# Gate stage of a streaming encoder layer: rows turned by VectorE, h added by accumulating loads, and a pair's finishing placed inside the next pair

## The chip, the cores and the metric

The kernel runs on one core of a Trainium2 chip. The metric is the device time in microseconds of one execution; the figure of a kernel is the median of its runs. A profile is one further execution, recorded by the hardware. The engines of the core are named as in the profile: PE (TensorE, matrix products; PEld its weight loads), DVE (VectorE), ACT (ScalarE), POOL (GpSimd) and SP (SyncE, which here only issues transfers). Each engine works through its own list of instructions in order and waits where an instruction needs another engine's result or a transfer.

## The reference

One layer for 2048 frames of a new stream and 32 frames of a running one, 1024 channels each, in fp32:

```
hn   = rmsnorm(x, g_mix);  proj = hn @ w_in
h    = x + concat(mixer_A(proj), mixer_B(proj)) @ w_out
gate = sigmoid(rmsnorm(h, g_ple) @ w_ple_gate)        # 1024 x 1024
h    = h + (p @ w_ple) * gate                         # p: 256 wide
y    = rmsnorm(h, g_final)
```

The change concerns only the last three lines, the gate stage, from the stored h to the result y.

## The kernel before

Frames lie in 16 tiles of 128 rows and a short one of 32 (`tiles`). Earlier stages leave three things in device memory: `h_d`, the rows h; `e_d`, the rows e = p @ w_ple (for tile 15 e is computed in the gate stage itself); and `g_d`, the gate's weights, already scaled by g_ple. The factor 1/rms of each row is kept on chip (`rs_h`) and goes in as the scale of the sigmoid.

The gate product works on **pairs** of tiles, eight pairs (i = 0, 2, ... 14; "pair one" is i = 0, "pair eight" is i = 14 and has its own function `last_pair`). Two tiles of rows are the upper and lower half of a 2 x 2 block matrix, the channels its left and right half, and the product with the 2 x 2 blocks of the weights is formed with seven block products in place of eight (Strassen-Winograd, function `seven`). The operands on the rows' side are four blocks of the turned rows (channels on the partitions) and four sums:

- a11, a12: left and right half of the upper tile; a21, a22: of the lower tile
- S1 = a21 + a22, S2 = S1 - a11, S3 = a11 - a21, S4 = a12 - S2

Each operand is split into a part that PE takes at its full rate (`fp32r`, cast by ACT, line 77: "the cast") and the rest (`subtract` on DVE, line 78: "the low part"). A block product is 12 matmuls of 128 x 512: four chunks of channels times three combinations of parts. `seven` runs them in the order 11, 12, S2, S1, S3, S4, 22 (the last is called T4 after its weight block) into three banks X, Y and Z: 11, S2, S3 and 22 all add on in bank X, S1 and S4 in Z, 12 in Y.

What is done with a bank between two products is given to `seven` as two functions, `carry` and `out` (`gate_ops`). `carry` copies a bank to SBUF (ACT, line 1302), `out` adds a copy to a bank (DVE, line 1310), applies the sigmoid (ACT), multiplies with e (DVE, line 1313) and adds to h (DVE, line 1314). Since X goes on being written, the next product into X has to wait until the copy or the addition from X is done; between a product into X and the next there is always a product into another bank. The places are named (tile, half): X gives (0,0) after 11 and 12, (1,1) after S3, (1,0) after T4; Z gives (0,1) after S4.

`done_g` finishes a tile: sum of squares by ACT (line 88), two steps on POOL for 1/rms (`rstd_of`, lines 69 and 73), scaling by DVE (line 1321), and the transfer of the rows to y, issued by POOL (line 1322). It is called after both tiles of the pair are through.

The rows' side of the next pair is prepared by `prep_g` in two steps that `seven` calls between its products. The two tiles of a pair are turned in two ways:

- upper tile, `turned`: rows loaded, re-ordered by ACT (two copies `ho`, line 1280), turned by PE in eight transposes of 128 x 128 into the two `tr` banks (`pth`, line 1282)
- lower tile, `turned_here`: loaded as 4 x 4 KB blocks by four transfers (line 1291) and turned in blocks of 32 x 32 by one DVE transpose (line 1293); the blocks are laid so that this gives whole columns

Loads go out on SP's queue. Rings of buffers: `xh` (three tiles of rows), `ya` (five), `cmb` (eight split operands, seven per pair), `st` (carries), `qa` (`ho`). A load waits for the last reader of its buffer, and all loads behind it on SP's queue with it. The framework that records the kernel orders the instructions of each engine by due times of its own, within their dependences: the lists that result differ from the order of the calls, and a small change can move instructions some distance away.

Ahead of pair one come the last products of e (line 102, tiles e_3 to e_16), beside which DVE and ACT form the sums of the gate's weights chunk by chunk (`weight_sums`, loads at line 1268, `wg_r`), and the short tile (`plain`, "gl"), whose rows are turned by PE as well (`pth_16`, low parts `gl`).

Of the kernel before, what the change touches and what calls it, by code (L numbers as in the profile page):

```python
# [12 lines left out]
ALU = mybir.AluOpType  # L13
PSUM = bass.MemoryType.PSUM

P = 128
# [10 lines left out]
NT = SEQ // P + 1  # L27
NH = D // 2
# [6 lines left out]
def trunk(ctx, tc, x_p, x_s, c_conv, c_pool, p_p, p_s, g_mix, w_in, conv_w, conv_b, pool_w,  # L35
          pool_scale, w_out, g_ple, w_gate, w_ple, g_fin, y_p, y_s, sc_p, sp_p, sc_s, sp_s):
    nc = tc.nc
# [6 lines left out]
    h_d = tc.dram_tile([T, D], F32, name="h_d")  # L44
# [41 lines left out]
    def sumsq(x, n, name, r=None, later=False):  # L86
        ssq = sm.tile([P, 1], F32, tag="ssq", name=f"ssq_{name}")
        ins = nc.scalar.activation(junk[:n], x[:n], AF.Square, accum_out=ssq[:n])  # L88
# [218 lines left out]
    def ring4(t, name):  # L307
        return t.tile([P, D], F32, tag="t", name=name)
# [15 lines left out]
    def load_rows(pool, name, i, pr, sa=None):  # L324
        r, n = tiles[i]
        t = ring4(pool, f"{name}_{i}")
        nc.sync.dma_start(t[:n], pr[r:r + n] if sa is None else rows_of(pr, sa, r, n))
        return t

    with ExitStack() as s1:  # L330
# [17 lines left out]
        def put(piece, src):  # L348

            split(piece[:, :, 0], piece[:, :, 1], src)  # L350
# [274 lines left out]
        second = second_block()  # L625
# [475 lines left out]
    with ExitStack() as s2:  # L1101
# [13 lines left out]
        def half_of(x, at, n=P):  # L1115
            return x[at[0]][:n, at[1] * NH:at[1] * NH + NH]
# [145 lines left out]
        W = sums_slots("wg")  # L1262
# [9 lines left out]
        def turned(i):  # L1272

            r, n = tiles[i]
            t = load_rows(ya, "hn", i, h_d).rearrange("p (q k c) -> p k q c", q=4, k=KC)
            out = []
            for half in range(2):
                pt = tbank(f"pth_{i}_{half}")
                o = qa.tile([P, KH, P], F32, tag="q", name=f"ho_{i}_{half}")
                nc.scalar.copy(o[:n].rearrange("p k (q c) -> p k q c", q=4), t[:n, half * KH:half * KH + KH])  # L1280
                for k in range(KH):
                    nc.tensor.transpose(pt[:, k * P:k * P + n], o[:n, k], ident[:n, :n])
                out.append(pt.rearrange("p (k t) -> p k t", k=KH))
            return out

        def turned_here(i):
# [6 lines left out]
            nc.vector.transpose(t, t)  # L1293
            u = t.rearrange("p (g k t) -> p k g t", g=4, k=KC)
            return u[:, :KH], u[:, KH:]

        def gate_ops(h, e, n, name, i):
            scale = lambda at: rs_h[:n, i + at[0]:i + at[0] + 1]

            def carry(ps, at):  # L1300
                t = st.tile([P, NH], F32, tag="t", name=f"c_{name}_{at[0]}{at[1]}")
                nc.scalar.copy(t[:n], ps[:n])
                return t

            def out(ps, c, at):
                if c is None:
                    c = st.tile([P, NH], F32, tag="t", name=f"g_{name}_{at[0]}{at[1]}")
                    nc.scalar.activation(c[:n], ps[:n], AF.Sigmoid, scale=scale(at))
                else:
                    nc.vector.tensor_tensor(c[:n], ps[:n], c[:n], op=ALU.add)  # L1310
                    nc.scalar.activation(c[:n], c[:n], AF.Sigmoid, scale=scale(at))
                ee, hh = half_of(e, at, n), half_of(h, at, n)
                nc.vector.tensor_tensor(ee, ee, c[:n], op=ALU.mult)
                nc.vector.tensor_tensor(hh, hh, ee, op=ALU.add)

            return carry, out

        def done_g(i, h):
            r, n = tiles[i]
            rf = sumsq(h, n, f"f{i}")  # L1320
            nc.vector.scalar_tensor_tensor(h[:n], h[:n], rf[:n], g_bc[:n], op0=ALU.mult, op1=ALU.mult)  # L1321
            nc.gpsimd.dma_start(rows_of(y_p, y_s, r, n), h[:n])

# [18 lines left out]
        def last_pair(i, A):  # L1342
# [63 lines left out]
            def second(half, m):  # L1406
                ps = bank(f"e_l{half}")
                embed_product(ps, pps, wp, slice(half * NH, half * NH + NH))
                finish(1, half, ps, m)

            pps = embedded()
            seven(f"g{i}", A, W, carry, out, {5: lambda: second(1, NH)}, first_tile=True)
            second(0, NH // 2)

        def prep_g(i):

            A = {}
# [12 lines left out]

            def first():
                lower.extend(turned_here(i + 1))

            def second():
                a21, a22 = lower
                s1 = comb("S1", a21, a22, ALU.add, whole)
                a11, a12 = turned(i)
                put("11", a11)
                s2 = comb("S2", s1, a11, ALU.subtract)
                s3 = comb("S3", whole(a11), a21, ALU.subtract, whole)  # L1440
                put("12", a12)
                put("S2", s2)
                s4 = comb("S4", a12, s2, ALU.subtract)
# [8 lines left out]
        S = {}  # L1452
        n = tiles[NT - 1][1]
        A = short("gl", turned(NT - 1), n)
        for step in prep_g(0).values():
            step()
        for c in range(len(rest_e) - LATE, len(rest_e)):
            run(c)
        h, e = (load_rows(*a) for a in ((xh, "h", NT - 1, h_d), (ya, "e", NT - 1, e_d)))
        plain("gl", A, W, n, *short_ops(h, e, n))  # L1460
        done_g(NT - 1, h)
        for i in range(0, NT - 3, 2):
            A = S.pop(i)
            h = [load_rows(xh, "h", i + b, h_d) for b in range(2)]
            e = [load_rows(ya, "e", i + b, e_d) for b in range(2)]
            seven(f"g{i}", A, W, *gate_ops(h, e, P, f"g{i}", i), prep_g(i + 2))
            for b in range(2):
                done_g(i + b, h[b])
        last_pair(NT - 3, S[NT - 3])


# [27 lines left out]
```

## Time and profile before

| | us |
|---|---|
| median of 3 runs (lowest to highest) | 945.34 (943.99 to 947.28) |
| the profiled execution, its own time | 942.12 |
| its span, first to last instruction | 940.3 |
| PE busy | 920.7 |
| DVE busy | 726.3 |
| ACT busy | 480.5 |
| POOL busy | 126.2 |
| gate pairs, from the first product to PE's last (windows) | 770.6 to 932.3 |

The span is what the profile can explain; the time lies about 1.8 us above it. Mean granted PE clock was 0.994. In the profile's rows, the columns are start, duration, engine, line, operation, and what was written from what; `x12` counts equal instructions; in brackets stands the engine's idle time before, and who ended it. In rows of groups it is busy time, mean ns, and idle time before. Windows give for each engine busy time and number of instructions, then PE's clock, the share of the transfer engines and GB/s.

### The profile page before, as it was taken

To read this page: it belongs to the slowest core of one execution; us is meant where nothing else is said; L and a number is where in the kernel's file an instruction comes from. 1 tells how busy PE (TensorE), PEld (TensorE's weight loads), DVE (VectorE), ACT (ScalarE), POOL (GpSimd) and SP (SyncE) were. 2 spreads that over 40 slices of the span, in tenths; PEclk is the share of its full clock that TensorE was granted. 3 is DMA by queue.
4 is the path that set the end of the run, shared out by engine and by line. 5 is a ranking of instruction groups with operands and counts; after the bars stand their busy time and mean duration, and the time that the engine had idled before them with its cause. 6 is when DMAs were issued, how large, how long until landed. Compare 5 with 4: busy or idle time off the path is not lost.

```text
span 940.3 us, 13055 instructions
## 1 busy us (share of the span) xinstructions
PE 920.7 (98%) x4599; PEld 831.5 (88%) x4599; DVE 726.3 (77%) x1230; ACT 480.5 (51%) x890; POOL 126.2 (13%) x244
## 2 busy tenths in 40 slices
PE   7999999999999999999999999999999999999996
PEld 5999999999999999999999987888878868888885
DVE  6697998899587978785777588765554797888985
ACT  5554555454444554443454356334334875555564
POOL 2101222120000110000000010211211001211113
PEclk8999999999999999999999999999999999999999
DMA  8336586696952655418655359865785883566653
GB/s 247 101 105 172 143 243 197 182 255 207 423 166 80 178 161 144 151 52 287 198 167 176 117 176 305 263 194 170 217 253 171 307 274 130 201 227 209 216 207 112
DMA packets 133214, 182.96 MB, mean 195 GB/s; under 512 B 11164, under 2 KB 105116, under 8 KB 131869
## 3 DMA queue, kind: packets, MB, share of 16 engines
q1 hardware_dynamic: 117165, 131.70, 45.2%
q0 software_dynamic: 13248, 44.93, 14.9%
q10 hardware_dynamic: 2736, 5.51, 1.8%
q8 instruction: 36, 0.59, 0.3%
q14 instruction: 29, 0.24, 0.1%
HBM read 127.23 MB, written 54.86 MB: 194 GB/s over the span
## 4 chain that ended last, share of the span: by engine, by line
PE 74%; DMA 3%; DVE 2%; ACT 2%; issue 0%; POOL 0%; POOLq 0%; DVEq 0%; ACTq 0%
PE x_o L167 9%; PE x_g L167 9%; PE e L102 5%; PE z_g L167 5%; PE x_zab L556 5%; PE z_o L167 4%; PE x_ch L556 4%; PE x_zbv L556 4%; PE z_zab L556 2%; PE y_g L167 2%; PE y_o L167 2%; PE b L556 2%; PE v L556 2%; PE zb L556 2%; PE za L556 2%; PE c L556 2%
## 5 line engine op out<-in xcount | busy, mean ns | idle before, releaser
L77 ACT CAST y_S<-y_fS 128x512 fp32r<-128x512 f32 x32 | 19.5, 621 | 42.5 <-PE x_o L167 18.9
L102 PE MATMUL e<-wq,pps 128*128 128x512 f32 (+1 forms) x156 | 38.8, 399 | 0.2 <-ACT pps L77 0.2
L406 DVE SCALAR_TENSOR_TENSOR xt<-xt,rstd_x,g_bc 128x1024 f32<-128x1024 f32 (+2 forms) x18 | 23.1, 1282 | 19.4 <-POOL rstd_x L73 18.0
L167 PE MATMUL x_g<-wg_b,g_S 128*128 128x512 f32 x128 | 35.9, 390 | 0.0
L167 PE MATMUL x_o<-wo_b,y_S 128*128 128x512 f32 x128 | 35.8, 391 | 0.0
L556 PE MATMUL z_ch<-B,w_ch_S 128*128 128x416 f32 x168 | 34.3, 352 | 0.9 <-ACT U L851 0.9
L556 PE MATMUL z_zab<-B,w_zab_S 128*128 128x416 f32 x168 | 34.1, 351 | 0.5 <-ACT U L851 0.5
L556 PE MATMUL x_zab<-B,w_zab_S 128*128 128x416 f32 x168 | 34.5, 352 | 0.1
L556 PE MATMUL z_zbv<-B,w_zbv_S 128*128 128x416 f32 x168 | 34.2, 352 | 0.0
L556 PE MATMUL x_zbv<-B,w_zbv_S 128*128 128x416 f32 x168 | 34.1, 351 | 0.0
L556 PE MATMUL x_ch<-B,w_ch_S 128*128 128x416 f32 x168 | 34.0, 351 | 0.0
L102 PEld LDWEIGHTS e<-wq,pps 128*128 128x128 f32 (+1 forms) x156 | 27.4, 182 | 6.9 <-ACT pps L77 0.5
L556 PEld LDWEIGHTS z_ch<-B,w_ch_S 128*128 128x128 f32 x168 | 31.2, 188 | 1.6 <-ACT U L851 1.2
L556 PEld LDWEIGHTS z_zab<-B,w_zab_S 128*128 128x128 f32 x168 | 31.3, 188 | 1.1 <-ACT U L851 0.8
L556 PEld LDWEIGHTS x_zab<-B,w_zab_S 128*128 128x128 f32 x168 | 31.2, 188 | 1.0 <-DVE w_zab_S L78 0.4
L556 PEld LDWEIGHTS x_ch<-B,w_ch_S 128*128 128x128 f32 x168 | 31.4, 188 | 0.3
L556 PEld LDWEIGHTS x_zbv<-B,w_zbv_S 128*128 128x128 f32 x168 | 31.3, 188 | 0.3
L556 PEld LDWEIGHTS z_zbv<-B,w_zbv_S 128*128 128x128 f32 x168 | 31.3, 188 | 0.4
L69 POOL TENSOR_SCALAR ms_f<-ssq_f 128x1 f32<-128x1 f32 (+1 forms) x15 | 8.8, 585 | 160.7 <-ACT junk L88 160.7
L77 ACT CAST y<-y 128x512 fp32r<-128x512 f32 x24 | 14.8, 618 | 29.4 <-PE x_o L167 13.8
L1321 DVE SCALAR_TENSOR_TENSOR h<-h,rstd_f,g_bc 128x1024 f32<-128x1024 f32 (+1 forms) x15 | 19.3, 1284 | 12.7 <-POOL rstd_f L73 12.7
L167 PEld LDWEIGHTS x_o<-wo_b,y_S 128*128 128x128 f32 x128 | 24.0, 188 | 5.0 <-ACT c_o L1125 0.3
(570 smaller groups left out, 2670.7 us busy)
## 6 DMA issues: line engine op xcount, KB each, us to landing
y<-y_d SPq DMA_DIRECT2D x16, 512.0 KB, 12.7
x<-in_x_prompt_dram SPq DMA_DIRECT2D x16, 512.0 KB, 9.7
h_d<-x SPq DMA_DIRECT2D x16, 512.0 KB, 4.5
h<-h_d SPq DMA_DIRECT2D x16, 512.0 KB, 3.6
xt<-in_x_prompt_dram SPq DMA_DIRECT2D x15, 512.0 KB, 12.7
e<-e_d SPq DMA_DIRECT2D x15, 512.0 KB, 5.9
out_dram<-h POOLq DMA_DIRECT2D x14, 512.0 KB, 3.0
p_dT<-T POOLq DMA_DIRECT2D x12, 512.0 KB, 6.2
```

Of the source, the lines that this page charges most:

```text
L69: nc.gpsimd.tensor_scalar(ms[:n], ssq[:n], scalar1=1.0 / D, scalar2=EPS, op0=ALU.mult, op1=ALU.add)
L77: ins = nc.scalar.copy(hi, src)
L102: nc.tensor.matmul(ps[:n], pps[:, a, k, :n], wp[k][b][:, cs], start=k + q == 0, stop=k == 1 and q == 2)
L167: nc.tensor.matmul(ps[:n], lhs[:, k, a, :n], w[b][:, k], start=start and k + q == 0, stop=k == KH - 1 and q == 2, skip_group_check=True)
L406: nc.vector.scalar_tensor_tensor(xt[:n], xt[:n], r[:n], g_bc[:n], op0=ALU.mult, op1=ALU.mult)
L556: nc.tensor.matmul(ps[:, :NB], lhs[:, k, x], b[:, k, y], start=start and k + q == 0, stop=stop and k == KH - 1 and q == 2, skip_group_chec ...
L1321: nc.vector.scalar_tensor_tensor(h[:n], h[:n], rf[:n], g_bc[:n], op0=ALU.mult, op1=ALU.mult)
```

## The change

Three things are done.

1. In pairs two to eight both tiles are loaded as blocks and turned by DVE (`blocks`, `turned_here`); only pair one (`here=False`) and the short tile keep PE's transposes. The block loads of both tiles are issued ahead of the loads of e, into ring `xh`.
2. h is no longer loaded for pairs one to seven. After the multiplication e x gate, h is added to the half tile by a transfer from `h_d` that adds to what lies in SBUF, issued by POOL (four per pair). The sums stand in the e tile then. The short tile and the last pair add h by DVE as before.
3. `done_g` of a pair is called inside the next pair, after its product S1 (step 4; in the last pair too).

```diff
+        def blocks(i):
             r, n = tiles[i]
-            t = ring4(ya, f"hn_{i}")
+            t = ring4(xh, f"hn_{i}")
             for q in range(4):
                 nc.sync.dma_start(...)
+            return t
+
+        def turned_here(t):
             nc.vector.transpose(t, t)
...
-                ee, hh = half_of(e, at, n), half_of(h, at, n)
+                ee = half_of(e, at, n)
                 nc.vector.tensor_tensor(ee, ee, c[:n], op=ALU.mult)
-                nc.vector.tensor_tensor(hh, hh, ee, op=ALU.add)
+                if h is None:
+                    r = tiles[i + at[0]][0]
+                    nc.gpsimd.dma_start(ee, h_d[r:r + P, at[1] * NH:at[1] * NH + NH], accum_op=ALU.add)
+                else:
+                    hh = half_of(h, at, n)
+                    nc.vector.tensor_tensor(hh, hh, ee, op=ALU.add)
...
-            rf = sumsq(h, n, f"f{i}")
+            rf = sumsq(h, n, f"f{i}", later=i < NT - 1)
...
-            seven(f"g{i}", A, W, carry, out, {5: lambda: second(1, NH)}, first_tile=True)
+            seven(f"g{i}", A, W, carry, out, {4: finished, 5: lambda: second(1, NH)}, first_tile=True)
...
-        def prep_g(i):
+        def prep_g(i, here=True):
...
-            lower = []
+            rows = [blocks(i + b) for b in range(1 - here, 2)]
+            upper = []
             def first():
-                lower.extend(turned_here(i + 1))
+                upper.extend(turned_here(rows[0]) if here else map(whole, turned(i)))
             def second():
-                a21, a22 = lower
+                a11, a12 = upper
+                put("11", a11, whole)
+                a21, a22 = turned_here(rows[-1])
                 s1 = comb("S1", a21, a22, ALU.add, whole)
-                a11, a12 = turned(i)
-                put("11", a11)
-                s2 = comb("S2", s1, a11, ALU.subtract)
-                s3 = comb("S3", whole(a11), a21, ALU.subtract, whole)
-                put("12", a12)
+                put("12", a12, whole)
+                s2 = comb("S2", whole(s1), a11, ALU.subtract, whole)
+                s3 = comb("S3", a11, a21, ALU.subtract, whole)
...
+        ready = []
+
+        def finished():
+            while ready:
+                done_g(*ready.pop(0))
+
         for i in range(0, NT - 3, 2):
             A = S.pop(i)
-            h = [load_rows(xh, "h", i + b, h_d) for b in range(2)]
+            steps = prep_g(i + 2)
             e = [load_rows(ya, "e", i + b, e_d) for b in range(2)]
-            seven(f"g{i}", A, W, *gate_ops(h, e, P, f"g{i}", i), prep_g(i + 2))
-            for b in range(2):
-                done_g(i + b, h[b])
+            seven(f"g{i}", A, W, *gate_ops(None, e, P, f"g{i}", i), {**steps, 4: finished})
+            ready.extend((i + b, e[b]) for b in range(2))
         last_pair(NT - 3, S[NT - 3])
```

In the changed kernel the lines lie some nine further down: the addition to a bank is line 1314, the multiplication 1317, the accumulating load 1320, the scaling 1330, the transfer to y 1331.

More of the change, by code (lines that the diff above doesn't have):

```diff
@@ L1284, in turned @@
             return out
-        def turned_here(i):
+        def blocks(i):
             r, n = tiles[i]
-            t = ring4(ya, f"hn_{i}")
+            t = ring4(xh, f"hn_{i}")
             for q in range(4):
@@ L1427, in comb @@
                 return t
-            lower = []
+            rows = [blocks(i + b) for b in range(1 - here, 2)]
+            upper = []
             def first():
-                lower.extend(turned_here(i + 1))
+                upper.extend(turned_here(rows[0]) if here else map(whole, turned(i)))
             def second():
-                a21, a22 = lower
+                a11, a12 = upper
+                put("11", a11, whole)
+                a21, a22 = turned_here(rows[-1])
                 s1 = comb("S1", a21, a22, ALU.add, whole)
-                a11, a12 = turned(i)
-                put("11", a11)
-                s2 = comb("S2", s1, a11, ALU.subtract)
-                s3 = comb("S3", whole(a11), a21, ALU.subtract, whole)
-                put("12", a12)
+                put("12", a12, whole)
+                s2 = comb("S2", whole(s1), a11, ALU.subtract, whole)
+                s3 = comb("S3", a11, a21, ALU.subtract, whole)
                 put("S2", s2)
-                s4 = comb("S4", a12, s2, ALU.subtract)
+                s4 = comb("S4", a12, whole(s2), ALU.subtract, whole)
                 put("S1", s1)
@@ L1454, in trunk @@
         A = short("gl", turned(NT - 1), n)
-        for step in prep_g(0).values():
+        for step in prep_g(0, here=False).values():
             step()
```

## The prediction

> **What bounds the kernel now.** I read the page's busy times, then the chain that ended last, then windows of the gate stage, then one pair's timeline.
>
> ```profile
> span 940.3 us, 13055 instructions
> PE 920.7 (98%) x4599; PEld 831.5 (88%) x4599; DVE 726.3 (77%) x1230; ACT 480.5 (51%) x890; POOL 126.2 (13%) x244
> 827.73:847.67 19.94, 19.94 (x94) 16.60 (x93) 17.43 (x27) 11.39 (x20) 3.36 (x6) 1.00 0.63 216
> 841.34 2.72 PE x_g L167 x12
> 844.06 0.68 PE z_g L167 x3
> 844.74 0.87 PE pth L1282 x8
> 845.62 2.06 PE z_g L167 x9
> ```
>
> TensorE (PE) is busy 98% of the span. In the gate stage it never pauses: in the window of one pair (19.94 us) PE is busy 19.94, VectorE (DVE) 17.43, ScalarE (ACT) 11.39, GpSimd (POOL) 3.36. The chain shows what a pair is: seven products of 2.72 us (19.04) and eight transposes `pth` of 0.87 us together. So PE sets the end here, and an edit pays by what it takes from PE, and costs by each wait that it gives PE. The profiled execution took 942.12 us, the median of the runs is 945.34; I form the change on the profiled run and put it on the median.
>
> **What is removed.** Pairs two to eight lose their `pth`: 7 x 0.87 = 6.1 us off PE, all on the path. This is the whole gain.
>
> ```profile
> L1280 ACT COPY ho<-hn 128x512 f32<-128x512 f32 x2 | 1.1, 622 | 0.0
> L1293 DVE STREAM_TRANSPOSE hn<-hn 128x1024 f32<-128x1024 f32 x1 | 1.2, 1236 | 0.0
> L1314 DVE TENSOR_TENSOR h<-h,e 128x512 f32<-128x512 f32 x4 | 2.7, 685 | 0.0
> hn<-h_d SPq DMA_DIRECT2D x24, 128.0 KB, 2.8
> out_dram<-hg POOLq DMA_DIRECT2D x1, 256.0 KB, 2.6
> L1322 POOL DMA_DIRECT2D out_dram<-h x2 | 1.1, 570 | 1.1 <-DVE h L1321 1.1
> ```
>
> Off the path, per pair: ACT loses two `ho` copies (1.1 us). DVE gains one transpose (1.2) and loses four additions (2.7). The loads of h (2 x 512 KB) give way to four accumulating loads of 256 KB, the row loads of the upper tile to block loads like the lower tile's, so about the same bytes move. POOL gains four issues of about 0.57 us (2.3 on 3.4 busy in some 20). None of these engines becomes the bound.
>
> The accumulating load is in no row. I take 2.6 us, POOL's other 256 KB transfer; the ends are 2.6 and 12.7, the slowest 512 KB load:
>
> ```profile
> y<-y_d SPq DMA_DIRECT2D x16, 512.0 KB, 12.7
> ```
>
> The last of a pair waits for the product T4 of that pair, a sigmoid and a multiplication: 2.7 + 0.2 + 0.7 + 0.7 and the issue of 0.57, some 5 us after T4 starts. The second sum of squares that reads it starts 15 us after T4 does (2.7 for T4, 1.8 for the rest of "11", three products, and 2.4, below). So 10 us are open to it, and up to there it costs nothing; nor can it gain, as no PE work is taken away by it. On POOL's queue an accumulating load waits for its multiplication; the one for half (0,0), the only one ahead of the means and roots, has its data 5 us before the first of these is due.
>
> **What is moved: the finishing of a pair.** This costs the time. In the instruction lists of the two kernels, each engine's order is fixed. Before, the squares (L88), POOL's root and the final scaling on DVE (L1321) run early in the next pair, ahead of that pair's addition for tile (1,1) (L1310). Now they are called after product S1, and in pairs four to seven the lists read:
>
> ```
> ACT   S3 cast (waits for PE: its buffer held S1)   carry of Z   squares   squares   S4 cast ...
> DVE   ... S3 low   scaling   scaling   S4 low   addition (1,1)   addition (0,1) ...
> PE    S1 | S3 | S4 | 4 matmuls of the next "11" | T4 (waits for addition (1,1), which reads its bank X)
> ```
>
> PE is in order, so T4 now waits behind two scalings. The price comes from the same steps in the trace before:
>
> ```profile
> 816.47 1.06 ACT L88 ACTIVATE junk<-h 128x1024 bf16<-128x1024 f32 x1 [1.96 <-DVE h L1314]
> 817.72 0.19 POOL L69 TENSOR_SCALAR ms_f<-ssq_f 128x1 f32<-128x1 f32 x1 [14.98 <-ACT junk L88]
> 818.58 1.28 DVE L1321 SCALAR_TENSOR_TENSOR h<-h,rstd_f,g_bc 128x1024 f32<-128x1024 f32 x1 [0.94 <-POOL rstd_f L73]
> 818.89 1.02 POOL L69 TENSOR_SCALAR ms_f<-ssq_f 128x1 f32<-128x1 f32 x1 [0.35 <-ACT junk L88]
> 820.58 1.29 DVE L1321 SCALAR_TENSOR_TENSOR h<-h,rstd_f,g_bc 128x1024 f32<-128x1024 f32 x1 [0.72 <-POOL rstd_f L73]
> 821.21 2.88 PE L167 MATMUL x_g<-wg_b,g_S 128*128 128x512 f32 x12
> 821.41 0.59 ACT L1302 COPY c_g<-z_g 128x512 f32<-128x512 f32 x1 [1.52 <-PE z_g L167]
> 821.78 0.69 DVE L1313 TENSOR_TENSOR e<-e,c_g 128x512 f32<-128x512 f32 x1
> 821.89 1.14 ACT L1280 COPY ho<-hn 128x512 f32<-128x512 f32 x2
> 784.29 0.69 DVE L1310 TENSOR_TENSOR c_g<-x_g,c_g 128x512 f32<-128x512 f32 x1 [1.26 <-PE x_g L167]
> 785.02 0.72 ACT L1311 ACTIVATE c_g<-c_g,rs_h 128x512 f32<-128x512 f32 x1 [1.84 <-DVE c_g L1310]
> 808.75 1.88 DVE L78 TENSOR_TENSOR g_S<-g_fS,g_S 128x512 fp32r<-128x512 f32 x3
> ```
>
> Let s be the end of S1 (the S3 product starts at 821.21). ACT reacts 0.20 later. S3 cast and carry take about 0.5 each (821.41 to 821.89 for one copy), so squares start at s + 1.2. From the first square to the second scaling: 816.47 to 820.58 = 4.11; that scaling holds DVE until 821.78, 1.20 more: s + 6.5. S4's low part takes 0.6 of DVE's queue (three in 1.88), the addition until its reader starts 0.73 (784.29 to 785.02): T4 may start at s + 7.84. PE has for cover S3, S4 and four matmuls: 2.72 + 2.72 + 0.91 = 6.35. PE waits 1.5 us in each of four pairs: **6.0**. Each pair starts from the last one's delay, and the steps in front (casts, first carry) have slack of over 2 us, so the wait neither grows nor is made up. It is 0.7 at least, if POOL's step `ms_f` takes 0.19 as at 817.72 and not 1.02; 2.3 if each of its two steps loses that 0.83 again.
>
> Here a row and a rule meet. `ms_f` takes 0.19 with DVE waiting and 1.02 under a scaling. The Trainium skill (SBUF — State Buffer, "Who interferes with whom") says that a VectorE instruction with two SBUF inputs contends with a GpSimd instruction that reads SBUF, and the 1.02 agrees. By the rule the 1.02 stays, since the same scaling runs beside it; without it the four waits would fall to 2.8 us in all.
>
> Pair two finishes pair one in another order: no cast ahead (squares at s + 0.7), but three forming steps (0.6 each) between scalings and addition, two of them behind the second. Scaling two ends at s + 6.0 to 6.3, the two steps 1.2, the addition 0.73: 8.0 to 8.2, against 2.72 + 2.72 + eight matmuls 1.81 = 7.25: **0.9** (0 to 1.5). Pair three has 12 + 6 matmuls ahead of T4, a cover of 9.5. Its second scaling stands behind four steps of DVE: first scaling s + 2.8 to 4.0, four steps to 6.4, scaling to 7.6, two steps to 8.8, addition 9.5: just in time, **0.3** (0 to 1).
>
> The finished rows now leave later too, and an e buffer of the 5-deep ring with them:
>
> ```profile
> out_dram<-h POOLq DMA_DIRECT2D x14, 512.0 KB, 3.0
> ```
>
> Issued at s + 5.9, landed at s + 8.9; there SP's load of a later e waits for the buffer, and behind it on SP's queue the four block loads of the next tile to be turned. These land by about s + 13.8 (2.1 to issue five, 2.8). DVE comes to that transpose after the next pair's product 12 and its first multiplication, at s + 17. Cover 3 us, price nothing; without it each us later would first eat the slack that DVE has ahead of S3's low part.
>
> **The last pair's tail.** Here the end hangs on DVE and ACT, not on PE:
>
> ```profile
> 921.16 1.07 PE L167 MATMUL x_g<-wg_b,g_S 128*128 128x512 f32 x4
> 921.36 0.59 ACT L1302 COPY c_g<-z_g 128x512 f32<-128x512 f32 x1 [1.13 <-PE z_g L167]
> 925.07 0.69 DVE L1399 TENSOR_TENSOR c_g<-z_g,c_g 128x512 f32<-128x512 f32 x1 [1.40 <-PE z_g L167]
> 927.76 0.68 DVE L1372 TENSOR_TENSOR h<-h,c_g 128x512 f32<-128x512 f32 x1
> 928.53 0.63 ACT L1374 ACTIVATE junk<-h 128x512 bf16<-128x512 f32 x1
> ```
>
> Squares of pair seven now follow the copy of 921.36: start 921.84, second scaling 925.95 to 927.15, where the addition of 925.07 now has to wait: 2.1 late. Both additions then run before the gate's multiplication, which used to have one between it and the sum of 927.76; 0.7 is won back: h is summed by 929.2 to 929.9, and the squares of 928.53 start at 929.9: **1.4** late, and all after it (0.5 to 2.5).
>
> **The start of the stage.** `pth` of pair one moves on PE from behind the short tile's product (765.08) into e_14's, and the low parts of the short tile on DVE from ahead of weight chunk three's sums to behind them.
>
> ```profile
> 756.59 5.73 PE e L102 x24
> 765.08 0.87 PE pth L1282 x8
> 757.57 0.28 DVE L78 TENSOR_TENSOR gl<-pth,gl 128x128 fp32r<-128x128 f32 x1
> 758.57 0.68 DVE L177 TENSOR_TENSOR wg_r<-wg_r,wg_r 128x512 f32<-128x512 f32 x1
> 754.37 0.32 SPq L1268 DMA_DIRECT2D wg_r<-g_d  x1
> 747.54 0.32 SPq L148 DMA_DIRECT2D e_d<-eout  x1
> 753.66 0.69 DVE L78 TENSOR_TENSOR wg_b<-wg_r,wg_b 128x512 fp32r<-128x512 f32 x1
> DMA to landing us min/median/max: 4.3/5.2/5.5
> ```
>
> `pth` takes the bank that `gl` (757.57) releases. Now `gl` stands behind the sum of 758.57: seven DVE steps of 0.6, that sum among them, a short `pps` and itself, 4.7 us. That sum needs the last weight load, which is issued earlier than at 754.37, since on SP's queue it passes two writes of e. It then waits for an earlier write (747.54) and for its buffer, whose last use was at 753.66 and comes earlier with the loads: I put it between, at 751. Landing takes 5 (the last row, of the tile `wg_r`): 756, and `gl` ends at 760.5. PE comes to `pth` nine matmuls (2.0) after 756.59, at 758.6: **1.9** of waiting, 0 to 4 (0 with the load at 749, 4 at 753).
>
> **Sum.** -6.1 + 1.9 + 0.9 + 0.3 + 6.0 + 1.4 = +4.4 us: 946.5 for the profiled run, 949.7 on the median.
>
> **Rivals.** (1) No new wait: the squares come early enough, DVE's 2.7 us less of additions carry the rest. Then -6.1: 939.2. For it: DVE has more slack than before on average. Against: an order, not a load, makes the wait; it needs squares by s - 0.3, and the S3 cast in front cannot start before s + 0.2. (2) Half-size waits: no 1.02 on POOL (2.8 for 6.0), the start's wait 0, the tail's 0.5: -6.1 + 2.8 + 1.2 + 0.5 = -1.6, 943.7; with one of the three undone, up to about +2: no change. (3) The accumulating loads land late. From 10 us on, ACT's queue (squares, then S4, 22, the sigmoids) stops, and DVE and PE behind it; at 12.7 us 2.7 us in each of six pairs, +16: 966. Against: transfers of POOL's queue of this size took 2.6. That the transposes stay on PE is excluded: the list of the changed kernel has none of the 56.
>
> **Numbers.** About 0.3%, 2.8 us, is what a measurement here can tell from no change. Forecast 0.57, own range 945.5 to 954; (1) 0.13; (2) 0.20; (3) 0.10. Slower holds the forecast but its lowest edge, and (3): 0.66. Same: most of (2) and that edge, 0.19. Faster: (1) and the low end of (2), 0.15. The range goes over (2) into (1), and to the largest ends of the terms above: 940.5 to 956.
>
> **What would show it.** Right: PE busy under 100% in gate windows; pairs four to seven at 20.5 us, the idle time in front of `x_g<-wg_T` released by DVE L1314; scalings of L1330 after S3 in each pair; a gap on PE at `pth`. Wrong: pairs of 19.04 (rival 1), squares waiting on a DMA (3), `ms_f` always near 0.2 (2).

## The result, and the profile after

The changed kernel took 955.85 us (median of 4, 953.19 to 957.47) where the kernel before took 944.66 in runs on the same chip: a ratio of 1.0121, 95% interval 1.0097 to 1.0145, slower by 11 us. A second set of runs (at the end of the experiments) gave 958.30 and 1.0154 (1.0126 to 1.0181). The forecast of 949.7 had the sign right; its change, +4.4 us, was less than half of the measured one.

The page of the changed kernel (span and busy times, two groups, one kind of transfer), and then a window over one of its pairs, from one first `y_g` to the next:

```profile
span 951.4 us, 13009 instructions
PE 918.2 (97%) x4543; PEld 824.3 (87%) x4543; DVE 718.9 (76%) x1209; ACT 473.3 (50%) x876; POOL 150.1 (16%) x272
L167 PE MATMUL x_g<-wg_T,g 128*128 128x512 f32 x96 | 24.1, 400 | 8.8 <-DVE c_g L1314 8.2
L1320 POOL DMA_DIRECT2D e<-h_d x28 | 24.7, 953 | 54.8 <-DVE e L1317 50.4
e<-h_d POOLq DMA_DIRECT2D x28, 256.0 KB, 6.6
```
```profile
857.21:877.93 20.72, 19.38 (x85) 15.69 (x84) 17.44 (x24) 10.47 (x18) 6.95 (x10) 1.00 0.75 200
```

PE lost the 56 transposes and 2.5 us of work, and yet a pair takes 20.72 us instead of 19.94: PE now stands idle 1.34 of them, and DVE, at 17.44, is no busier than it was. The page's third row says where: 8.8 us idle ahead of T4 in the whole stage, 8.2 of them ended by DVE's addition. Its last two rows are the accumulating load, 0.95 us of issue on POOL and 6.6 us to landing.

Where the 11 us are is read from two instructions that both kernels share: the short tile's product in the stage before (`x_ol`), and the first `y_g` of pair one. In PE's timeline, the kernel before and then the changed one:

```profile
695.34 1.08 PE L270 MATMUL x_ol<-wo_c,yl 128*64 128x512 f32 x4
773.14 0.39 PE L167 MATMUL y_g<-wg_c,g 128*128 128x512 f32 x1
913.00 0.39 PE L167 MATMUL y_g<-wg_c,g 128*128 128x512 f32 x1
```
```profile
692.49 1.08 PE L270 MATMUL x_ol<-wo_c,yl 128*64 128x512 f32 x4
775.46 0.39 PE L167 MATMUL y_g<-wg_c,g 128*128 128x512 f32 x1
919.54 0.39 PE L167 MATMUL y_g<-wg_c,g 128*128 128x512 f32 x1
```

(The third row is the first `y_g` of pair eight.) The differences, with the second profile of the changed kernel beside the first:

| stretch | before | changed | again | change | forecast |
|---|---|---|---|---|---|
| up to `x_ol`, untouched | 695.3 | 692.5 | 697.8 | -2.9, +2.4 | 0 |
| `x_ol` to pair one | 77.8 | 83.0 | 83.5 | +5.2, +5.7 | +1.9 |
| pair one to pair eight | 139.9 | 144.1 | 143.8 | +4.2, +3.9 | +1.1 |
| pair eight to the end of the span | 27.3 | 31.9 | 33.0 | +4.6, +5.7 | +1.4 |

The first row is scatter, and it goes both ways: the first profiled execution was ahead of the profile of before by 2.9 us before it came to anything changed. The changed stage costs 14 us in the first profile and 15 in the second, against the forecast's 4.4; the forecast put each of the three stretches too low.

**The pairs.** In pair seven's loop the chain is the forecast one, step by step:

```profile
906.79 2.88 PE L167 MATMUL x_g<-wg_b,g_S 128*128 128x512 f32 x12
907.99 1.06 ACT L88 ACTIVATE junk<-e 128x1024 bf16<-128x1024 f32 x1
909.23 0.19 POOL L69 TENSOR_SCALAR ms_f<-ssq_f 128x1 f32<-128x1 f32 x1 [4.35 <-ACT junk L88]
910.10 1.28 DVE L1330 SCALAR_TENSOR_TENSOR e<-e,rstd_f,g_bc 128x1024 f32<-128x1024 f32 x1 [1.76 <-POOL rstd_f L73]
910.46 0.97 POOL L69 TENSOR_SCALAR ms_f<-ssq_f 128x1 f32<-128x1 f32 x1 [0.40 <-ACT junk L88]
912.10 1.29 DVE L1330 SCALAR_TENSOR_TENSOR e<-e,rstd_f,g_bc 128x1024 f32<-128x1024 f32 x1 [0.72 <-POOL rstd_f L73]
913.90 0.69 DVE L1314 TENSOR_TENSOR c_g<-x_g,c_g 128x512 f32<-128x512 f32 x1
914.64 3.02 PE L167 MATMUL x_g<-wg_T,g 128*128 128x512 f32 x12 [1.33 <-DVE c_g L1314]
```

S3 starts at 906.79, squares 1.2 later, the second scaling ends at 913.4, the addition follows S4's low part, T4 comes 7.85 after S3's start (forecast 7.84). For the accumulating loads ScalarE's squares waited four times (total, times, longest):

```profile
ACT junk L88 <- DMA e<-h_d: 3.5, 4, 1.8
```

Two of the four waits, 0.36 and 1.76 us, are in pair three, and there they count. The last load of pair two is issued some 6.4 us after that pair's T4 starts and takes 9.5 us to land (the median of all is 6.6). The second squares wait for it, ScalarE's casts and VectorE's second scaling stand behind them, and T4 is late:

```profile
827.57 1.06 ACT L88 ACTIVATE junk<-e 128x1024 bf16<-128x1024 f32 x1 [1.76 <-DMA e<-h_d]
834.82 3.03 PE L167 MATMUL x_g<-wg_T,g 128*128 128x512 f32 x12 [1.68 <-DVE c_g L1314]
```

A wait of 1.34 us costs a pair 1.68 (20.72 against 7 x 2.72 = 19.04), since PE is also busy 0.34 longer.

**The start.** PE stops one step earlier in its list than forecast:

```profile
756.61 0.22 DVE L78 TENSOR_TENSOR pps<-ptp,pps 128x64 fp32r<-128x64 f32 x1
756.88 0.43 PE L1282 MATMUL pth<-ident,ho 32*128 32x32 f32 x4 [3.40 <-DVE pps L78]
```

The short tile's own second transpose waits 3.40 us for a `tr` bank, whose reader, the low part of `pps_16`, stands behind the weight sums in DVE's list. The stretch grew by more than this wait. In windows from `x_ol` to pair one, the kernel before and then the changed one, PE is also busy 1.77 us longer, and its granted clock (1.00 is full speed) falls:

```profile
695.34:773.14 77.80, 77.56 (x359) 57.77 (x358) 55.48 (x92) 50.66 (x99) 4.79 (x11) 1.00 0.75 251
692.49:775.46 82.97, 79.33 (x359) 58.91 (x358) 55.24 (x92) 50.23 (x98) 4.79 (x11) 0.98 0.64 213
757.24 3.92 PE L102 MATMUL e<-wq,pps 128*128 128x512 f32 x10
```

The third row is the work right behind the wait: ten matmuls take 3.92 us, where the kernel before needs 5.80 for 24. The granted clock there is 0.50 to 0.66 for some 4 us, from 757.8 on. So the 5.17 us are 3.40 of waiting and 1.77 of slower work; in the second profile they are 3.88 and 1.81.

**The last pair.** ScalarE waits twice for chunks of w_ple. Counted from pair eight's first `y_g`, they are issued little later than before: 3.7 and 1.0 us ahead of it in place of 5.3 and 1.2. But they take 7.6 us to land, not 3.3. The landing from the view of the tile `wlr`, before and changed; then SyncE's row of before; then the timeline of SyncE, ScalarE, PE and VectorE in the changed kernel:

```profile
DMA to landing us min/median/max: 3.3/3.3/3.3
DMA to landing us min/median/max: 7.6/7.6/7.6
```
```profile
907.72 4.42 SPq L1239 DMA_DIRECT2D wlr<-in_w_ple_dram  x2
```
```profile
915.86 2.99 SPq L1239 DMA_DIRECT2D wlr<-in_w_ple_dram  x2
920.97 1.05 ACT L77 CAST wl<-wlr 128x1024 fp32r<-128x1024 f32 x1 [2.58 <-DMA wlr<-in_w_ple_dram]
926.22 1.05 ACT L77 CAST wl<-wlr 128x1024 fp32r<-128x1024 f32 x1 [3.72 <-DMA wlr<-in_w_ple_dram]
930.67 3.04 PE L167 MATMUL z_g<-wg_d,g_S 128*128 128x512 f32 x12 [1.06 <-ACT c_g L1306]
934.92 1.29 DVE L1330 SCALAR_TENSOR_TENSOR e<-e,rstd_f,g_bc 128x1024 f32<-128x1024 f32 x1 [0.72 <-POOL rstd_f L73]
936.12 0.68 DVE L1408 TENSOR_TENSOR c_g<-z_g,c_g 128x512 f32<-128x512 f32 x1
```

Z's copy on ScalarE stands behind the second cast, so S4 starts late; and the addition that reads S4 (done when the product behind it starts, 933.55) waits for the second scaling as well, 2.4 us. In the second profile the chunks take 8.6 us, ScalarE waits 7.3 us for them, and PE's granted clock falls once more (0.58 and 0.56 from 937.1 to 941.1).

### The profile page after: what moved, and what is told of

Read it like the earlier page. It is cut to its first block, busy times and chain, and to the rows that moved or that the text cites. A ratio compares the mean times of both kernels' runs of the same rounds, so it can differ in the third digit from the quotient of the medians.

```text
span 951.4 us, 13009 instructions
## 1 busy us (share of the span) xinstructions
PE 918.2 (97%) x4543; PEld 824.3 (87%) x4543; DVE 718.9 (76%) x1209; ACT 473.3 (50%) x876; POOL 150.1 (16%) x272
## 3 DMA queue, kind: packets, MB, share of 16 engines
q0 software_dynamic: 17280, 52.27, 19.2%
## 5 line engine op out<-in xcount | busy, mean ns | idle before, releaser
L77 ACT CAST y_S<-y_fS 128x512 fp32r<-128x512 f32 x32 | 19.5, 622 | 43.1 <-PE x_o L167 19.9
L1320 POOL DMA_DIRECT2D e<-h_d x28 | 24.7, 953 | 54.8 <-DVE e L1317 50.4
L167 PE MATMUL x_g<-wg_T,g 128*128 128x512 f32 x96 | 24.1, 400 | 8.8 <-DVE c_g L1314 8.2
L167 PEld LDWEIGHTS x_g<-wg_T,g 128*128 128x128 f32 x96 | 17.5, 188 | 15.2 <-DVE c_g L1314 10.8
L1330 DVE SCALAR_TENSOR_TENSOR e<-e,rstd_f,g_bc 128x1024 f32<-128x1024 f32 x14 | 18.0, 1284 | 16.7 <-POOL rstd_f L73 16.7
```

What stands on the lines that cost most here:

```text
L77: ins = nc.scalar.copy(hi, src)
L167: nc.tensor.matmul(ps[:n], lhs[:, k, a, :n], w[b][:, k], start=start and k + q == 0, stop=k == KH - 1 and q == 2, skip_group_check=True)
L1320: nc.gpsimd.dma_start(ee, h_d[r:r + P, at[1] * NH:at[1] * NH + NH], accum_op=ALU.add)
```

## The experiments

The theory: waits made by the order of VectorE's and ScalarE's lists, and by rings that are held longer, cost the time. Its rivals: the accumulating loads cost it as transfers, or VectorE's longer list does as load. All runs have the kernel before beside them on the same chip; ratios are to it. Line numbers of edited kernels shift by a few.

**e1: one scaling in mid-pair, the other ahead of T4.**

```diff
-            seven(..., {**steps, 4: finished})
+            seven(..., {**steps, 4: one, 6: one})     # one: done_g of the next finished tile
```

> The changed kernel with one edit: of the two finished tiles of a pair, only the first is squared and scaled in the middle of the next pair; the second follows ahead of that pair's last product (T4). Theory (the two scalings stand ahead of the addition (1,1) in VectorE's list, and T4 waits for it): with one scaling of 1.29 us ahead instead of two the addition comes about 2 us earlier, so the wait of 1.3 us ahead of T4 and the slow restart behind it go in six pairs, 6 x 1.5 = 9 us; the tiles of the last finished pair are written about 5 us later, which may give 1 to 2 us back at the end: 946 to 949 us. Rival (the loss lies in the accumulating loads and the DMA traffic, or in VectorE's load as such): the order does not matter, 954 to 957 us.

952.17 us, ratio 1.0105 (1.0091 to 1.0119). Between the two theories: the wait ahead of T4 is gone in pair two and falls to 0.5 to 0.6 us in pairs three to five and to 0.25 in seven, so in these the order makes most of it; but pair six waits 1.66, for another wait comes in. PE's row of pair five, and SyncE's and VectorE's rows behind it:

```profile
870.45 3.03 PE L167 MATMUL x_g<-wg_T,g 128*128 128x512 f32 x12 [0.55 <-DVE c_g L1314]
874.55 2.52 SPq L1291 DMA_DIRECT2D hn<-h_d  x4
885.86 1.25 DVE L1297 STREAM_TRANSPOSE hn<-hn 128x1024 f32<-128x1024 f32 x1 [3.96 <-DMA hn<-h_d]
```

VectorE stands 4 us at a transpose whose blocks, issued up to 877.1, take 8.8 us more to land, beside accumulating loads.

**e2: w_ple's chunks in unused buffers.**

```diff
-                raw = ring4(ya, ...)                       # 4 KB, ring of e
+                raw = [qa.tile([P, NH], ...) for g in range(2)]   # last pair; loads ahead of e's
```

> The changed kernel with one edit: the two chunks of w_ple that the last pair splits are loaded as halves into the two small buffers that the last pairs leave unused, instead of into the ring of embedding tiles, so that the first chunk doesn't wait for finished tiles; the second chunk is loaded once the first is split. Theory (ScalarE waits 2.6 and 3.7 us for these chunks in the last pair, and z's product S4, the squares and everything behind them follow): the last pair gets 2 to 4 us shorter, 952 to 954 us. Rival (the last pair is long because its accumulating loads land late or because its list of finishing work is longer): within 1 us of the changed kernel, 955 to 957 us.

955.64 us, ratio 1.0136 (1.0122 to 1.0150): no gain, the theory's number missed. The first chunk was there early, but the second, loaded only when the first was split, came at 928.16 after 6.78 us of waiting on ScalarE (926.22 and 3.72 above). One late chunk is as bad as two. The edit did not take the suspect away, so it decides nothing.

**e3: pair one prepared in the old order.**

```diff
-            return {2: first, 3: second}
+            return {2: first, 3: second} if here else {2: first_low, 3: second_low}   # as before
```

> The changed kernel with one edit: pair one alone is prepared in the order of the kernel before (lower tile turned first and its sum S1 made first, then the upper tile through TensorE). Theory (the start of the gate stage costs about 5 us, since TensorE's transposes stand behind low parts that VectorE does late): 3 to 5 us less, 951 to 953 us. Rival (the start is late because the blocks of h are loaded behind other transfers, whatever the order on VectorE): less than 1 us, 955 to 957 us.

954.92 us, ratio 1.0118 (1.0102 to 1.0134): nothing gained, and `x_ol` to pair one is 83.3 us in its profile. The order in which pair one is prepared is not what costs the start. VectorE's list showed it: weight sums still stood ahead of the `pps`.

**e4: e1, e2 and e3 together.**

> The three edits together: one scaling in mid-pair and one ahead of T4, w_ple's chunks in the unused small buffers, pair one prepared in the old order. Theory: the three savings lie in different stretches and add up, 955.9 - 9 - 3 - 4 = 940 us, between 938 and 944, and so 1 to 6 us faster than the kernel before. Rival (waits are only pushed elsewhere: the next thing late is the accumulating loads): 948 us or more.

951.00 us, ratio 1.0091 (1.0070 to 1.0112). The savings did not add up to 16 us; the start still cost 84.1 us from `x_ol` to pair one. The theory as it stood, order alone, has failed in its sizes.

**e5: pair one's block in the old ring.** What e3 left: the change also moved the block tiles from ring `ya` to `xh`, the ring through which the gate's weights pass.

```diff
-        def blocks(i):                            t = ring4(xh, f"hn_{i}")
+        def blocks(i, pool=xh):                   t = ring4(pool, f"hn_{i}")
+            rows = [blocks(i + b, xh if here else ya) ...]
```

> The changed kernel with one edit: the block tile of pair one alone lies in the ring of embedding tiles (ya), where it lay before, and not in the ring (xh) through which the eight tiles of the gate's weights pass. VectorE's list up to the preparation of pair one is then the list of the kernel before, low parts of the embeddings ahead of the weight sums. Theory (the shared ring makes the planner draw the weight sums forward, TensorE's transposes wait 3.4 us at a bank whose reader stands behind them, and the gate stage starts 5 to 6 us late): 5 to 6 us less than the changed kernel, about 950 us, a ratio to the kernel before of 1.005 to 1.007. Rival (the start is late for a reason that the old order of preparing pair one didn't touch either, the loads of the blocks): less than 1.5 us, ratio 1.010 or more.

952.09 us, ratio 1.0100 (1.0086 to 1.0115): over the ratio that the theory gave, and at the rival's edge. But in PE's timeline the start is whole again:

```profile
697.64 1.08 PE L270 MATMUL x_ol<-wo_c,yl 128*64 128x512 f32 x4
775.44 0.39 PE L167 MATMUL y_g<-wg_c,g 128*128 128x512 f32 x1
758.20 0.68 PE L1282 MATMUL pth<-ident,ho 32*128 32x32 f32 x8
```

77.80 us, that of before to the hundredth, and `pth` without a wait; 5.2 to 5.7 us of the loss were a choice of ring. In the ratios to the kernel before it is 2 us against the first set of runs of the changed kernel and 5 against the second, so the size rests on the profiles.

**e6: finishing after the pair (third part undone).**

```diff
-            seven(..., {**steps, 4: finished})
-            ready.extend((i + b, e[b]) for b in range(2))
+            seven(..., steps)
+            for b in range(2):
+                done_g(i + b, e[b])
```

> The changed kernel with its third part undone: both rows of a pair are squared, scaled and written after the pair's own last product, as before; the turning by VectorE and the accumulating loads stay. Theory (the accumulating load lands 6.6 us after its issue, and what is called right behind it waits that long): the scalings stand at the start of the next pair in VectorE's list, ahead of the sums for S2 and S4, and hold it 4 to 6 us; TensorE waits 2 to 4 us in each of seven pairs, 965 to 980 us. Rival (finishing in mid-pair is itself what costs, whatever it waits for): T4 no longer waits, 945 to 948 us.

983.57 us, ratio 1.0420 (1.0403 to 1.0437), a little over the upper end. ScalarE and PE in turn:

```profile
856.81 1.06 ACT L88 ACTIVATE junk<-e 128x1024 bf16<-128x1024 f32 x1 [5.93 <-DMA e<-h_d]
858.49 0.79 PE L167 MATMUL x_g<-wg_a,g_S 128*128 128x512 f32 x1 [4.14 <-ACT c_g L1306]
```

So landing is free only while nobody stands behind it: with the squares called right after it, ScalarE stops, VectorE's scaling behind it (7.31 us in this pair), and PE. The third part of the change is the price of the second.

**e7: h added by VectorE (second part undone).**

```diff
-            t = ring4(xh, f"hn_{i}")
+            t = ring4(ya, f"hn_{i}")
+            h = [load_rows(xh, "h", i + b, h_d) for b in range(2)]
-            seven(..., *gate_ops(None, e, ...), {**steps, 4: finished})
+            seven(..., *gate_ops(h, e, ...), {**steps, 4: finished})    # finishes h
```

> The changed kernel with its second part undone: h is loaded as a tile of its own and added by VectorE (four additions of 0.69 us in a pair), embedding tiles are free as soon as they are multiplied, and the blocks lie in their ring again; the turning by VectorE and the finishing in mid-pair stay. Theory (the start and the last pair lose by rings that are held, the pairs by two scalings ahead of the addition (1,1)): the start's 5 to 6 and the last pair's 3 us come back, the waits ahead of T4 stay at 1.3 us or grow with VectorE's longer list, up to 2.5 us in each of six pairs: 947 to 954 us. Rival (the accumulating loads cost most of it, as transfers): 940 us.

947.75 us, ratio 1.0052 (1.0034 to 1.0069), in the theory's range. `x_ol` to pair one is 77.8 us, and pairs take 20.1 to 20.9 from pair three on, with waits ahead of T4 and no accumulating load anywhere. But the last pair's loss stayed, against the theory. PE's row of pair seven's T4:

```profile
914.51 3.01 PE L167 MATMUL x_g<-wg_T,g 128*128 128x512 f32 x12 [0.64 <-DVE c_g L1314]
```

From it to the end of the span it takes 31.0 us, and 30.0 in the kernel before (from 910.28), although 14 matmuls of pair eight (3.2 us) that come after T4 there come ahead of it here. So the last pair is some 4 us too long without any accumulating load, and with waits of 1.8 us in all for w_ple's chunks.

**e8: the turning alone.**

```diff
 (e7, and)
-            seven(..., {**steps, 4: finished})
+            seven(..., steps)
+            for b in range(2):
+                done_g(i + b, h[b])       # after the pair, as before
```

> The kernel before with the first part of the change alone: in pairs two to eight the upper tile, too, is turned by VectorE; h is added by VectorE and the rows are finished after their pair, as before. Theory (what the change wins is TensorE's 7 x 0.87 us, and all that it loses comes from the second and third part and the ring they take): 6 us less than the kernel before, less up to 2 for one more turning of 1.24 us in VectorE's list: 938 to 941 us where the kernel before takes 944.7, a ratio of 0.993 to 0.996. Rival (VectorE's longer list, two turnings of 1.24 us a pair, makes TensorE wait by itself): no faster than before, ratio 0.999 or more.

937.95 us, ratio 0.9945 (0.9931 to 0.9959): faster than both kernels, by 5 us than before. One pair in a window:

```profile
850.44:869.48 19.04, 19.04 (x86) 15.77 (x84) 18.29 (x27) 10.67 (x19) 3.40 (x6) 1.00 0.72 225
```

A pair is 7 x 2.72 = 19.04 us, PE never idle, with VectorE busy 18.29 of it. VectorE's load as such makes no wait in it; the first part of the change gives nearly what the forecast gave it (pair one to pair eight takes 134.4 us, 5.4 less than before). This kernel and e7 differ only in when a pair is finished. So finishing it inside the next pair costs some 10 us (1.0052 against 0.9945) without any accumulating load, and 3 to 4 of them lie in the last pair, which takes 27.9 us here from its first `y_g` to the end (27.3 before).

**e9: e7 with both scalings behind the additions.**

```diff
-            seven(..., {**steps, 4: finished})
+            seven(..., {**steps, 6: finished})
```

> The run with h added by VectorE and rows finished in mid-pair (947.75 us, pairs every 20.5 to 20.6 us), with one edit: the finishing is called ahead of the pair's last product instead of after its fourth, so that both scalings stand behind the additions (1,1) and (0,1) in VectorE's list. Theory (T4 waits for the addition (1,1) behind the two scalings, and nothing else is wrong with finishing late): the waits ahead of T4, 0.3 to 0.7 us, and their restarts go; pairs every 19.1 to 19.4 us, 938 to 941 us. Rival (what counts is that work of one pair is carried into the next at all, with rings held longer): 945 us or more.

953.37 us, ratio 1.0108 (1.0085 to 1.0131), a clear miss. T4 still waits, in the profile of the fastest run (949.34 us) too:

```profile
867.94 1.89 DVE L1323 TENSOR_TENSOR h<-h,e 128x512 f32<-128x512 f32 x3
872.15 0.68 DVE L1314 TENSOR_TENSOR c_g<-x_g,c_g 128x512 f32<-128x512 f32 x1
872.89 3.02 PE L167 MATMUL x_g<-wg_T,g 128*128 128x512 f32 x12 [0.81 <-DVE c_g L1314]
876.70 1.28 DVE L1330 SCALAR_TENSOR_TENSOR h<-h,rstd_f,g_bc 128x1024 f32<-128x1024 f32 x1 [0.86 <-POOL rstd_f L73]
```

The scalings are behind the addition, as meant, but there VectorE stalls for their roots (0.86 us, and 0.44 for the second), and with some 18 us of work a pair (18.29 in e8's window) it falls behind: additions to h stand in front of the next addition (1,1), three of them in the first row. How much each does was not taken apart.

**e10: accumulating loads with three edits: e5, e2, and finishing ahead of T4.**

> The changed kernel, accumulating loads and all, with three edits: pair one's block in the old ring, both rows finished ahead of the pair's last product, w_ple's chunks in the unused small buffers. Theory (with the accumulating loads an embedding tile stays in its ring of five until its rows are written, so later finishing means later loads, and SyncE's queue holds the blocks of h behind the load that waits for a tile): the start's 6 us come back, the waits ahead of T4 go, and waits for blocks of 3 to 5 us on VectorE take their place in some pairs: 944 to 950 us, still slower than before. Rival (order alone decides): 938 to 941 us, as fast as the turning alone.

946.41 us, ratio 1.0033 (1.0016 to 1.0050), as the theory had it: 8 to 11 us better than the changed kernel and slower than before. No T4 wait is left in the profile; three pair distances are 19.04 us, the others 19.5 to 20.5, and the last pair takes 33.1 us from its `y_g` to the end, with PE waiting for a copy behind a late w_ple chunk:

```profile
922.84 1.20 PE L167 MATMUL x_g<-wg_b,g_S 128*128 128x512 f32 x4 [2.81 <-ACT c_g L1314]
```

The same move as in e9 works here. The two kernels differ in VectorE's 2.7 us of additions a pair and in the rings; that the former decides is likely and was not tried by itself.

**e11: plain loads in place of accumulating ones.** The loads overwrite the tile with h, so the sum of h and gate x e is left out in these rows.

```diff
-                    nc.gpsimd.dma_start(ee, h_d[...], accum_op=ALU.add)
+                    nc.gpsimd.dma_start(ee, h_d[...])
```

> The changed kernel with the adding left out of its 28 accumulating loads: the same bytes come by the same queue at the same places into the same tiles, as plain loads, so that the gate's product is overwritten by h (the sum h + gate x e is left out of these rows). All lists of instructions are the same. Theory (the accumulating loads are waited for in few places, but take the DMA engines about twice as long as plain ones): landing 2.5 to 4 us instead of 6.6, POOL's issue 0.6 instead of 0.95 us, DMA share back to that of before; the T4 waits of 1.33 us stay, the last pair's w_ple chunks land sooner and win 2 to 3 us: 952 to 954 us. Rival 1 (they cost nothing but their own landing): 955 to 957 us. Rival 2 (most of the loss is theirs): below 948 us.

952.81 us, ratio 1.0107 (1.0085 to 1.0129). The T4 waits of pairs four to seven stay (1.35), but no square waits for a load any more, and pair three's T4, which waited 1.68 and 1.66 in the changed kernel, runs without a wait from the same lists. From pair eight's `y_g` to the end it takes 29.5 us instead of 31.9 and 33.0. Pair three's T4, the changed kernel's queue on its page, then this one's queue and load, then the landing of this one's w_ple chunks:

```profile
838.47 3.02 PE L167 MATMUL x_g<-wg_T,g 128*128 128x512 f32 x12
```
```profile
q0 software_dynamic: 17280, 52.27, 19.2%
```
```profile
q0 software_dynamic: 15488, 52.27, 17.4%
e<-h_d POOLq DMA_DIRECT2D x28, 256.0 KB, 4.8
```
```profile
DMA to landing us min/median/max: 5.0/5.0/5.0
```

A queue's columns are packets, MB and the share of 16 engines. The chunks land in 5.0 us where they took 7.6, and ScalarE waits 3.6 us for them in place of 6.3. So 2.4 to 3.5 us of the last pair's loss come with the adding; that they come by its longer use of the transfer engines is likely. 2.2 us (29.5 against 27.3) are left, for the scalings and for chunks that still land later than before. In e7 the finishing costs more than that with no such load at all, so the split holds for this kernel only.

**e12: the changed kernel again.**

> The changed kernel once more, unedited, for a second profile and a tighter median, since the first profile was 2.85 us ahead of the profile of before at a point that the change doesn't touch. Theory (that lead is scatter; the start of the gate stage, the waits ahead of T4 and the last pair are the loss): the product that ends the stage before (x_ol) at 695 to 698 us instead of 692.5, from there to the short tile's first gate product 71 to 74 us where the kernel before has 66.8, waits ahead of T4 of 1.2 to 2 us in six pairs, and 955 to 957 us in all, a ratio of 1.011 to 1.014. Rival (the first run's medians were off, and the changed stage costs less than its profile says): a ratio under 1.010.

958.30 us, ratio 1.0154 (1.0126 to 1.0181), slightly more than expected; the first profile's lead was scatter. The rows of PE's timeline behind the table's column (the span is 958.1 us):

```profile
697.75 1.08 PE L270 MATMUL x_ol<-wo_c,yl 128*64 128x512 f32 x4
781.26 0.39 PE L167 MATMUL y_g<-wg_c,g 128*128 128x512 f32 x1
925.07 0.39 PE L167 MATMUL y_g<-wg_c,g 128*128 128x512 f32 x1
```

## Why the prediction was right in its direction and wrong in its size

- **The removed transposes, -6.1.** Right. e8 has pairs of 19.04 us, 5.4 us less from pair one to pair eight, and a ratio of 0.9945.
- **Pairs four to seven, +6.0.** Right in mechanism and nearly in size: 1.68 each, 6.7. `ms_f` took 0.19 ahead of the first scaling and 0.97 beside it, so the rule cited from the Trainium skill (SBUF — State Buffer, "Who interferes with whom") held here and the rival without that step is out. What was missed is that PE is busy 0.34 longer a pair around the wait.
- **Pairs two and three, +0.9 and +0.3.** Too small: what is left of the stretch is 4.2 + 6.1 - 6.7 = 3.6 in place of 1.2. Pair two's T4 waited 1.18 and 0.91, near its term, and each wait brings some longer PE time with it, as in pairs four to seven. Pair three's T4, "just in time", waited 1.68 us in the first profile and 1.66 in the second. The step that failed there is "up to there it costs nothing": the squares waited for an accumulating load, and with plain loads (e11) the wait is gone. The load was issued 6.4 us after T4's start, some 2 later than forecast, and landed 9.5 later, where the squares were ready after 14.3.
- **The start, +1.9 with 4 as its upper end.** The step that failed is which wait ends last. The forecast let PE stop at the bank that `gl` releases; PE stopped one step earlier, at the bank of `pps_16`. The list that the forecast read had `pps` behind the sums, but it priced `gl` alone (and its own figures give 760.7 for the end of `gl`, not 760.5). The wait itself, 3.40 and 3.88, is still under 4; what takes the stretch to +5.2 and +5.7 is PE's slower clock behind the wait, 1.8 us for which the forecast has no term. The cause of the new order was not seen either: the diff's `ring4(xh, ...)`, shown by e3 (order of preparation: no effect) and e5 (ring: all of it).
- **The last pair, +1.4 with 2.5 as its upper end.** Measured +4.6 and +5.7. The late second scaling is there as forecast (2.4 us, forecast 2.1). The step that failed is that an accumulating load costs nothing but its own landing: w_ple's chunks, issued at nearly the same places, land in 7.6 us in place of 3.3 and stop ScalarE for 6.3 us, and with plain loads the pair is 2.4 to 3.5 us shorter. The delay by held e buffers, priced at nothing, is small here too (1.6 and 0.2 us). And the 0.7 "won back" does not show: 2.2 us remain in e11. How the whole divides stays open: e2 did not free the chunks, and without accumulating loads (e7 against e8) the finishing alone costs 3 to 4 us here.
- **The accumulating load, 2.6 us, free up to 10.** The price was wrong (6.6 us, up to 9.5 where pair three needs it). That it is free in mid-pair held in most pairs and failed in pair three; rival 3 as it stood, 2.7 us in each of six pairs, is out. What was left out is that it holds up other loads. Without the adding, e11 is 1.3 us (1.0107 against 1.0121) to 4.4 us (against 1.0154) faster, with intervals that overlap.
- **The range.** 955.85 lies at its very end. Rivals 1 and 2 asked for smaller waits, and the loss came by the forecast's own terms, of which three (the start, pairs two and three, the last pair) were about three times too small or more. Its upper end was meant to be put together from bounds of terms (they add up to +12.1, which is 957.4 and not 956), each of a wait that was named; what was not named (the slower clock behind a wait, loads held up by other loads) was in none of them.

## What to carry to other kernels

A ring is part of an edit: when a tile moves to another ring, list who else passes through the old and the new one, at the first and at the last iteration too, and read whether the planner's lists change there; one ring name cost 5 us here. Undo a change of three parts one part at a time before giving it up: one part alone was 5 us faster than before, and the two others, with the ring that came along, cost 17 to 20 us on top of it. Price a wait in an in-order list from the engine's whole list in that stretch. Where a step comes "just in time", ask which transfer it stands behind, and take that transfer's landing from rows beside other traffic. When a new transfer is added, list which other loads run beside it.

## What the hardware showed that was not expected

An accumulating transfer of 256 KB on POOL's queue landed in a median of 6.6 us (7.0 in the second profile), where the plain one in the same place took 4.8. It took POOL a median of 885 ns to issue against 540. It moved in 64 packets more each (17280 - 15488 = 28 x 64), and the queue's share of the transfer engines rose from 17.4% of 952.7 us to 19.2% of 951.4, 16.9 us over 28 transfers: 0.6 us more of all 16 engines for each. And a wait of PE costs more than its length: 1.34 us idle made a pair 1.68 us longer at a granted clock of 1.00. At the start of the stage PE's granted clock fell to 0.50 behind the waits of 3.40 and 3.88 us, and behind 3.25 in e1; behind the same wait in e2, 2.04 us, it stayed at 1.00. Length alone does not decide it: in e6 it stayed at 1.00 behind a wait of 3.32 us (952.3). What else does was not tried.
